# Output projection: norm factors moved from the operand to the products, and weight-block sums made early and kept in DRAM

## The chip, the cores and the metric

The kernel runs on one core of one Trainium2 chip. The metric is the device time of one execution in microseconds (us). The core has a matrix engine (TensorE, PE in the profile), a vector engine (VectorE, DVE), an activation engine (ScalarE, ACT), a general engine (GpSimd, POOL) and SyncE (SP), whose queue issues all of this kernel's DMA transfers. Each engine works through its own instructions in order and waits on semaphores for the others.

## The reference

One layer of a decoder trunk in float32: 2048 tokens, model width 1024. An input projection feeds two parallel mixers, a diagonal state-space layer with a GLU (`y_a`) and an SSD mixer (`y_b`). Each result is RMS-normalised with a gain per channel, the two are joined, and one output projection of 2048 channels maps them back to 1024. An FFN follows. The part that the change touches is the middle of this:

```python
y_a = rmsnorm(y_a, s5_norm[i])
...
y_b = rmsnorm(y_b, ssd_norm[i])
x = x + jnp.concatenate([y_a, y_b], axis=-1) @ w_out[i]
h = rmsnorm(x, norm_ffn[i])
x = x + (jax.nn.silu(h @ w_gate[i]) * (h @ w_up[i])) @ w_down[i]
```

`rmsnorm(y, g)` multiplies each token's row by one number, `rsqrt(mean(y*y) + eps)`, and each channel by its gain `g`.

## The kernel before

**Products.** Float32 products are made of three matmuls of a split operand: each operand is rounded to a high part (a copy on ACT, line 942) and the remainder is the low part (a subtraction on DVE, line 947); `split` does both. The output projection and the FFN use Winograd's form of Strassen's scheme on 2x2 blocks: seven products P1 to P7 instead of eight. For one step, `stationary_operands` makes seven operands from the token side (A11, A12, A22 and the sums S1 to S4, four sums on DVE), each 128 channels by 128 tokens in four pieces. The weight side, `Moving`, keeps seven operands (B11, B21, B22 and the sums T1 to T4) of 4 x 128 channels by 512 columns, which serve eight steps. A step is 7 x 4 x 3 = 84 matmuls of 128x128 by 128x512, all recorded at line 1126.

**The output projection, `mixed_out`.** It runs 16 steps: r = 0, 1 over the two halves of the channels (r=0 is `y_a`, read from DRAM as `yaD`; r=1 is `y_b`, `ybD`), and within each, c = 0 to 7 over groups of 256 tokens. `normed(r, c)` loads the raw tokens of the step after the present one, channels on partitions, puts the tokens' norm factors on a diagonal (`dg`, line 1173), spreads them over the partitions by a matmul with ones (`ps_iv`, line 1175), and multiplies by gain and factor with eight DVE instructions of 128x256 (line 1179). `winograd` then issues the products. Ends (line 1132) add a finished product from PSUM into the residual rows; a product that is needed further on in the same PSUM bank is first copied out by ACT (`kept`, line 1137) into one of two scratch tiles and added from there (line 1139). The first step of a row block uses another order of products, `FIRST`, than the others, `ORDER`. For r=0 the residual rows come from the input `x` and the sums go to DRAM (`xaD`); for r=1 they are loaded from `xaD`, whose rows are spread over all eight steps of r=0, and go on to the FFN.

**Weights of the output projection.** Four blocks of 1 MB of `w_out` are loaded for each r, and T1 to T4 are made of them on DVE (line 985 through `Moving.minus`, and lines 1197 and 1198 at the start). For r=0 this takes place at the start of `mixed_out`, for r=1 in `next_rows`: it loads two blocks at c=4, and hangs the rest on the products of c=7, after which the places of old operands come free. At r=1, c=4 `NextTokens` begins to prepare the operands of the FFN in half of the token buffer, which has one place for tokens from there on instead of two.

**Around it.** The GLU (`glu`) of the state-space layer ends just before: for each block of its output, ACT squares it and POOL adds the square to `sums` (line 921), from which `glu_norm` makes the norm factors `ainv` with ones-column matmuls (line 874). The SSD mixer gives `yinv` in the same way. The tiles of the output projection lie in memory that the SSD mixer's tiles leave.

**Far earlier,** at 195 to 420 us of the profiled execution, `project` runs the first half of the input projection's columns for the convolution (`xs`, 12 tiles) and the gate (`zs`, 8 tiles), two tiles in a pair. Each tile loads 0.5 MB of weights, splits them on ACT (line 66) and POOL (line 69) and has 48 matmuls; three PSUM banks take turns, and ACT evacuates them (line 718). DVE has the convolution (line 731) and, until about 240 us, the tables of the state-space layer. The five large buffers (`slots`, `k.take`) are not all in use then: number 3 is idle.

The order of each engine's instructions is set by a scheduler that lays the program out along a simulated timeline; `high_priority` and `issue_after` guide it.

Of the kernel before, what the change touches and what calls it, by code (L numbers as in the profile page):

```python
# [19 lines left out]
P = 128  # L20
# [860 lines left out]
def glu(k, ins, half, sp):  # L881
# [18 lines left out]
    for i in range(0, KD, 2):  # L900
# [5 lines left out]
        for q, (m, w, b) in enumerate(order):  # L906
# [13 lines left out]
            if m:  # L920
                nc.gpsimd.tensor_add(sums[:, b], sums[:, b], sq)
            if half and i + q == 1:
# [177 lines left out]

def winograd(k, A, B, order, scratch, C, onto, after={}):

# [10 lines left out]
    if "P4" not in chain:  # L1113
        kept["P7"] = (c21, c21)

    ends = {"P2": (c11, c21), "P3": (c12, c12), "P7": (c22, c22), "P4": (c21, c21)}
    bank = {}
    for name in order:
# [11 lines left out]
        if name in ends and (onto or name != "P4" or name not in chain):  # L1130
            dst, src = ends[name]
            V.tensor_add(dst, ps, dst if onto else src)  # L1132
            ps = None
        if name in kept:
            dst, block = kept[name]
            dst = scratch() if onto else dst
            nc.scalar.copy(dst, bank[root])  # L1137
            if onto:
                V.tensor_add(block, block, dst)  # L1139
# [4 lines left out]


def mixed_out(k, ins, sp, s):


    nc = k.nc
    V, G = nc.vector, nc.gpsimd  # L1150
    w_out = ins["w_out"][0]
    tok = lambda ap, hf, j: ap[hf * HALF : hf * HALF + HALF, :].rearrange("(c j) d -> j c d", j=8)[j]

    def load_of(r):
        def load(dst, i, j):
            row = r * D + i * 512
            nc.sync.dma_start(dst, w_out[row : row + 512, j * 512 : j * 512 + 512].rearrange("(k p) d -> p k d", p=P))

        return load

# [3 lines left out]

    def normed(r, c, behind=None):

        st = stage[:, c % 2 if r == 0 or c < 4 else 0].rearrange("p (k t) -> p k t", t=256)
        src = k.ybD[:, c * 256 : c * 256 + 256] if r else k.yaD[:, c, :]
        nc.sync.dma_start(st, src.rearrange("(k p) t -> p k t", p=P))
        dg = sp.tile([P, 2, P], F32, name="dg", tag="sq", bufs=1)  # L1170
        inv = k.yinv if r else k.ainv
        for i in range(2):
            V.tensor_scalar(dg[:, i], k.ident, inv[:, 2 * c + i : 2 * c + i + 1], None, MUL)
        ps = (k.px)([P, 256], "ps_iv")
        nc.tensor.matmul(ps, k.ones, dg.rearrange("p a b -> p (a b)"), start=True, stop=True)
        col = C_SSDN if r else C_S5N
        with k.tc.issue_after(behind) if behind else nullcontext():
            for kk in range(KD):
                V.scalar_tensor_tensor(st[:, kk], st[:, kk], k.cols[:, col + kk : col + kk + 1], ps, op0=MUL, op1=MUL)  # L1179
        return st  # L1180
# [4 lines left out]
    with k.tc.high_priority():  # L1185
        B = Moving(k, 4)
        x, y = (k.take(i, [P, 2, 4, 512], F32) for i in (s[0], 6))
        r11, r12, r22, r21 = x[:, 0], x[:, 1], y[:, 0], y[:, 1]
        load(r11, 0, 0)
        load(r12, 0, 1)  # L1190
        st = normed(0, 0)
        B.split("B11", 7, r11)
        t1 = B.split("T1", 8, r11, B.minus(r11, r12, r11))
        A = operands(st, True)
        load(r22, 1, 1)
        with k.tc.issue_after(k.last_sum):
            V.tensor_sub(r11, r22, r11)
            V.tensor_sub(r12, r22, r12)
        load(r21, 1, 0)
        B.split("T2", s[1], r11)  # L1200
        B.split("B22", s[2], r22)
        with k.tc.issue_after(t1[0]):
            B.split("B21", s[3], r21)
            B.split("T3", s[4], r12)
        t4 = B.split("T4", s[0], r21, B.minus(r21, r21, r11))
    k.spare = 6

    for r in range(2):
        after = {}
        for c in range(8):  # L1210
            first = r + c == 0
            if not first:
                A = operands(st, c == 0)
            if c < 7 or r == 0:
                st = normed(*divmod(r * 8 + c + 1, 8), t4[1] if first else None)
            if c == 4:
                if r:
                    ahead = NextTokens(k, 0, tile)
                else:
                    nextB, ops = next_rows(k, B, 4, load_of(1))  # L1220
            if c == 7:
# [7 lines left out]
            winograd(k, A, B, FIRST if c == 0 else ORDER, lambda: sp.tile([P, 512], F32, name="sg", bufs=2), [(t[:, 0], t[:, 1]) for t in xt], True, after)  # L1229
            for i in range(2):  # L1230
# [113 lines left out]
def trunk_kernel(ctx, tc, ins, out, dbg=None, upto="all"):  # L1344
# [21 lines left out]
    k.m2D = dp.tile([P, NG, P], F32, name="m2D")  # L1366
    k.m1D = dp.tile([P, NG, P], F32, name="m1D")
    k.qD = dp.tile([P, NG, P], F32, name="qD")

# [48 lines left out]
    with ExitStack() as c1:  # L1418
# [110 lines left out]
```

## Time and profile before

| | us |
|---|---|
| median of 3 runs | 3020.07 (3012.84 to 3021.89) |
| the profiled execution, its own time | 3016.45 |
| its span in the profile | 3014.7 |
| PE busy | 2833.0 (94%) |
| DVE busy | 2102.2 (70%) |
| ACT busy | 1118.2 (37%) |
| POOL busy | 535.6 (18%) |
| DMA | 398.84 MB, mean 132 GB/s |

Times within the profile are counted from its first instruction. "Idle before" is time that an engine stood still, and the name behind the arrow is what ended it. The matmuls overlap: one of 128x512 is shown with 389 ns, and the next starts well before it ends, so a PE that is busy all the time may still be held to its own pace and not by anything else. PEclk is the clock granted to PE, as a share of the full one. The output projection takes the time from 1279 us to about 1650 us.

### The profile page before, as it was taken

To read this page: it belongs to the slowest core of one execution; us is meant where nothing else is said; L and a number is where in the kernel's file an instruction comes from. 1 tells how busy PE (TensorE), PEld (TensorE's weight loads), DVE (VectorE), ACT (ScalarE), POOL (GpSimd) and SP (SyncE) were. 2 spreads that over 40 slices of the span, in tenths; PEclk is the share of its full clock that TensorE was granted. 3 is DMA by queue.
4 is the path that set the end of the run, shared out by engine and by line. 5 is a ranking of instruction groups with operands and counts; after the bars stand their busy time and mean duration, and the time that the engine had idled before them with its cause. 6 is when DMAs were issued, how large, how long until landed. Compare 5 with 4: busy or idle time off the path is not lost.

```text
span 3014.7 us, 35741 instructions
## 1 busy us (share of the span) xinstructions
PE 2833.0 (94%) x12972; PEld 2257.6 (75%) x12972; DVE 2102.2 (70%) x3953; ACT 1118.2 (37%) x1817; POOL 535.6 (18%) x462
## 2 busy tenths in 40 slices
PE   4898999999999989989899999999999999999996
PEld 3776777677787777768677788887788887878875
DVE  5586218989668888797878755556655557677686
ACT  3134322333454333332434433334333334243343
POOL 1343311114366766510000000000000000000000
PEclk8999999999999999999999999999999999999998
DMA  6455335443446454545455222233222224545444
GB/s 118 116 157 169 117 97 173 140 140 104 132 129 191 145 165 140 174 153 172 134 167 161 74 75 82 84 112 101 96 84 84 79 76 141 194 168 192 165 153 140
DMA packets 331992, 398.84 MB, mean 132 GB/s; under 512 B 49804, under 2 KB 249592, under 8 KB 331816
## 3 DMA queue, kind: packets, MB, share of 16 engines
q1 hardware_dynamic: 331816, 396.56, 42.1%
q8 instruction: 102, 1.67, 0.2%
q14 instruction: 74, 0.61, 0.1%
HBM read 264.39 MB, written 132.12 MB: 132 GB/s over the span
## 4 chain that ended last, share of the span: by engine, by line
PE 62%; DVE 19%; DMA 11%; issue 3%; ACT 2%; SPq 2%; POOL 1%; DVEq 0%; ACTq 0%; POOLq 0%
PE ps_w L1126 40%; PE ps_in L81 4%; PE ps_in L83 4%; PE ps_in L82 4%; DMA s<-ybD 2%; DVE s L947 2%; DVE acc L731 1%; DMA out_dram<-x 1%; PE ps_y L575 1%; DVE wS L947 1%; PE ps_glu L81 1%; PE ps_glu L82 1%; PE ps_glu L83 1%; DVE x L1132 1%; DVE s L1179 1%
## 5 line engine op out<-in xcount | busy, mean ns | idle before, releaser
L1126 PE MATMUL ps_w<-s,wS 128*128 128x512 f32 x3936 | 957.7, 397 | 39.0 <-DVE s L947 16.8
L1126 PEld LDWEIGHTS ps_w<-s,wS 128*128 128x128 f32 x3936 | 747.3, 191 | 213.9 <-DVE s L947 18.8
L1126 PE MATMUL ps_w<-s,wA 128*128 128x512 f32 x2952 | 731.4, 398 | 29.8 <-DVE x L1132 10.3
L1126 PEld LDWEIGHTS ps_w<-s,wA 128*128 128x128 f32 x2952 | 558.8, 190 | 167.7 <-DVE x L1132 12.1
L81 PE MATMUL ps_in<-s,whi 128*128 128x512 f32 x896 | 353.5, 395 | 9.1 <-ACT xp L718 9.0
L83 PE MATMUL ps_in<-s,wlo 128*128 128x512 f32 x896 | 351.8, 395 | 1.6 <-POOL wlo L69 1.6
L82 PE MATMUL ps_in<-s,whi 128*128 128x512 f32 x896 | 352.9, 394 | 0.0
L942 ACT CAST wS<-sum 128x512 fp32r<-128x512 f32 (+1 forms) x336 | 203.5, 611 | 396.7 <-PE ps_w L1126 195.6
L947 DVE TENSOR_TENSOR wS<-sum,wS 128x512 fp32r<-128x512 f32 (+1 forms) x336 | 225.5, 675 | 140.5 <-ACT wS L942 139.9
L69 POOL TENSOR_TENSOR wlo<-wst,whi 128x1024 fp32r<-128x1024 f32 x72 | 188.7, 2621 | 424.1 <-ACT whi L66 424.0
L942 ACT CAST wA<-s 128x512 fp32r<-128x512 f32 (+1 forms) x252 | 150.7, 610 | 242.0 <-PE ps_w L1126 162.1
L81 PEld LDWEIGHTS ps_in<-s,whi 128*128 128x128 f32 x896 | 169.4, 189 | 49.0 <-ACT xp L718 10.3
L83 PEld LDWEIGHTS ps_in<-s,wlo 128*128 128x128 f32 x896 | 169.4, 189 | 40.9 <-issue 3.1
L82 PEld LDWEIGHTS ps_in<-s,whi 128*128 128x128 f32 x896 | 169.4, 189 | 36.9 <-issue 2.3
L1132 DVE TENSOR_TENSOR gu<-ps_w,gu 128x512 f32<-128x512 f32 x134 | 92.5, 691 | 148.3 <-PE ps_w L1126 144.5
L803 POOL TENSOR_TENSOR s<-cm,dtas 128x512 fp32r<-128x512 f32 x128 | 161.8, 1292 | 76.0 <-PE ps_seg L804 76.0
L947 DVE TENSOR_TENSOR wA<-s,wA 128x512 fp32r<-128x512 f32 (+1 forms) x252 | 165.1, 671 | 3.2 <-ACT wA L942 3.2
L1132 DVE TENSOR_TENSOR x<-ps_w,x 128x512 f32<-128x512 f32 x160 | 108.7, 685 | 57.1 <-PE ps_w L1126 56.9
L731 DVE SCALAR_TENSOR_TENSOR acc<-xp,cols,acc 128x1024 f32<-128x1024 f32 x72 | 102.7, 1426 | 50.6 <-ACT acc L729 49.9
L66 ACT CAST whi<-wst 128x1024 fp32r<-128x1024 f32 x72 | 75.5, 1049 | 167.9 <-PE ps_in L82 99.8
L1137 ACT COPY gu<-ps_w 128x512 f32<-128x512 f32 x134 | 78.4, 586 | 141.7 <-PE ps_w L1126 141.4
L1139 DVE TENSOR_TENSOR x<-x,sg 128x512 f32<-128x512 f32 x125 | 85.0, 686 | 65.7 <-ACT sg L1137 38.5
(354 smaller groups left out, 3612.8 us busy)
## 6 DMA issues: line engine op xcount, KB each, us to landing
wst<-in_w_in_dram SPq DMA_DIRECT2D x56, 512.0 KB
s<-in_w_gate_dram SPq DMA_DIRECT2D x22, 1024.0 KB
s<-in_w_up_dram SPq DMA_DIRECT2D x22, 1024.0 KB
actD<-gu SPq DMA_DIRECT2D x44, 512.0 KB
s<-actD SPq DMA_DIRECT2D x16, 1024.0 KB
xD<-xo SPq DMA_DIRECT2D x24, 512.0 KB
uD<-ev SPq DMA_DIRECT2D x16, 512.0 KB
zD<-sz SPq DMA_DIRECT2D x32, 256.0 KB
```

The lines of the kernel that those rows point to most:

```text
L69: eng.tensor_sub(lo, st, hi.bitcast(F32))
L81: nc.tensor.matmul(ps, wh[:, i, :], rh[:, i, :], start=(i == 0), stop=False)
L82: nc.tensor.matmul(ps, wh[:, i, :], rl[:, i, :], start=False, stop=False)
L83: last = nc.tensor.matmul(ps, wl[:, i, :], rh[:, i, :], start=False, stop=(i == n - 1))
L731: V.scalar_tensor_tensor(acc, tap(i), col(i), acc, op0=MUL, op1=ADD)
L803: G.tensor_mul(r, bc(k.tri.unsqueeze(1), [P, 4, P]), bc(part, [P, 4, P]))
L942: a = k.nc.scalar.copy(op[:, 0], raw)
L947: b = eng.tensor_sub(op[:, 1, part], raw[:, part], op[:, 0, part].bitcast(F32))
L1126: nc.tensor.matmul(ps, a[:, p, i, :], b[:, q, i, :], start=(root == name and i == 0 and p + q == 0), stop=(i == n - 1 and p == 1), skip_gr ...
L1132: V.tensor_add(dst, ps, dst if onto else src)
L1137: nc.scalar.copy(dst, bank[root])
L1139: V.tensor_add(block, block, dst)
```

## The change

1. `normed` becomes `tokens`: it only loads. The token operands are made of raw tokens.
2. The norm factor of a token is applied as the products leave PSUM, where tokens lie on partitions: `winograd` gets `scale`, a factor per partition for each of the two token blocks, in the ends (a scaled add instead of an add) and in the kept copies (a scaled activation instead of a copy).
3. The channel gains go into the weights. `out_rows` loads two rows of blocks of `w_out` (0.5 MB each), scales them in place on ACT, makes T1 to T4 on DVE and stores all eight results, 2 MB, to DRAM (`woD`). It is called eight times, behind the six pairs of `xs` tiles and the first two pairs of `zs` tiles, with buffer 3, so that each call's loads wait for the store of the call before.
4. `mixed_out` loads its operands of the weight side, sums too, from `woD`: seven of 1 MB for each r instead of four blocks. `made_rows` replaces `next_rows` for r=1, with the loads of T3, T2, B22, B21 and T4 in its hooks of step c=7.
5. The last four additions of squares in the GLU of the second half are done by DVE instead of POOL.

```diff
@@ glu @@
             if m:
-                nc.gpsimd.tensor_add(sums[:, b], sums[:, b], sq)
+                (V if half and i == KD - 2 else nc.gpsimd).tensor_add(sums[:, b], sums[:, b], sq)
@@ winograd @@
-def winograd(k, A, B, order, scratch, C, onto, after={}):
+def winograd(k, A, B, order, scratch, C, onto, after={}, scale=None):
...
+    row = {"P2": 0, "P3": 0, "P7": 1, "P4": 1}
+    row_kept = {"P1": 0, "P6": 0, "P5": 1, "P7": 1}
...
-            V.tensor_add(dst, ps, dst if onto else src)
+            if scale:
+                V.scalar_tensor_tensor(dst, ps, scale[row[name]], dst, op0=MUL, op1=ADD)
+            else:
+                V.tensor_add(dst, ps, dst if onto else src)
...
-            nc.scalar.copy(dst, bank[root])
+            if scale:
+                nc.scalar.activation(dst, bank[root], AF.Identity, scale=scale[row_kept[name]])
+            else:
+                nc.scalar.copy(dst, bank[root])
@@ new functions @@
+OPS = ("B11", "B12", "B21", "B22", "T1", "T2", "T3", "T4")
+def out_rows(k, w_out, r, kk):
+    nc, V = k.nc, k.nc.vector
+    t = k.take(3, [P, 8, 512], F32)
+    for i in range(2):
+        b = t[:, 2 * i : 2 * i + 2].rearrange("p a n -> p (a n)")
+        row = r * 8 + i * 4 + kk
+        nc.sync.dma_start(b, w_out[row * P : row * P + P, :])
+        nc.scalar.activation(b, b, AF.Identity, scale=k.cols[:, C_S5N + row : C_S5N + row + 1])
+    b11, b12, b21, b22, t1, t2, t3, t4 = (t[:, i] for i in range(8))
+    V.tensor_sub(t1, b12, b11)
+    V.tensor_sub(t2, b22, t1)
+    V.tensor_sub(t3, b22, b12)
+    V.tensor_sub(t4, b21, t2)
+    nc.sync.dma_start(k.woD[r, kk], t)
+def made_rows(k, old, load):
+    m = Moving(k, 4)
+    x = k.spare
+    t = k.take(x, [P, 2, 4, 512], F32)
+    load(t[:, 0], "B11")
+    load(t[:, 1], "T1")
+    r = {}
+    def p1():
+        m.split("B11", old.at["B11"], t[:, 0])
+        load(t[:, 0], "T3")
+    def p2():
+        k.spare = old.at["B21"]
+        r["y"] = k.take(k.spare, [P, 2, 4, 512], F32)
+        load(r["y"][:, 0], "T2")
+        load(r["y"][:, 1], "B22")
+    def p6():
+        m.split("T1", old.at["T2"], t[:, 1])
+        load(t[:, 1], "B21")
+    def p5():
+        m.split("T2", old.at["T1"], r["y"][:, 0])
+        load(r["y"][:, 0], "T4")
+    def p4():
+        m.split("B21", old.at["T4"], t[:, 1])
+        m.split("T4", x, r["y"][:, 0])
+    return m, { ... "P7": split of "B22", "P3": split of "T3" ... }
@@ mixed_out @@
-    def normed(r, c, behind=None):
+    def tokens(r, c):
...
         nc.sync.dma_start(st, src.rearrange("(k p) t -> p k t", p=P))
-        dg = sp.tile([P, 2, P], F32, name="dg", tag="sq", bufs=1)
-        inv = k.yinv if r else k.ainv
-        for i in range(2):
-            V.tensor_scalar(dg[:, i], k.ident, inv[:, 2 * c + i : 2 * c + i + 1], None, MUL)
-        ps = (k.px)([P, 256], "ps_iv")
-        nc.tensor.matmul(ps, k.ones, dg.rearrange("p a b -> p (a b)"), start=True, stop=True)
-        col = C_SSDN if r else C_S5N
-        with k.tc.issue_after(behind) if behind else nullcontext():
-            for kk in range(KD):
-                V.scalar_tensor_tensor(st[:, kk], st[:, kk], k.cols[:, col + kk : col + kk + 1], ps, op0=MUL, op1=MUL)
         return st
...
-        t1 = B.split("T1", 8, r11, B.minus(r11, r12, r11))
+        B.split("T1", 8, x[:, 1])
         A = operands(st, True)
-        load(r22, 1, 1)
-        with k.tc.issue_after(k.last_sum):
-            V.tensor_sub(r11, r22, r11)
-            V.tensor_sub(r12, r22, r12)
-        load(r21, 1, 0)
-        B.split("T2", s[1], r11)
...
-        t4 = B.split("T4", s[0], r21, B.minus(r21, r21, r11))
+        load(x[:, 0], "T3")
+        load(x[:, 1], "B21")
+        B.split("T2", s[1], y[:, 0])
+        load(y[:, 0], "T4")
+        B.split("B22", s[2], y[:, 1])
+        B.split("T3", s[4], x[:, 0])
+        B.split("B21", s[3], x[:, 1])
+        t4 = B.split("T4", s[0], y[:, 0])
...
-                    nextB, ops = next_rows(k, B, 4, load_of(1))
+                    nextB, ops = made_rows(k, B, load_of(1))
@@ trunk_kernel @@
-        project(k, 0, h, xs)
+        todo = [(r, kk) for r in range(2) for kk in range(4)]
+        for _ in project_pairs(k, 0, h, xs):
+            out_rows(k, ins["w_out"][0], *todo.pop(0))
...
-            project(k, 0, h, zs)
+            for _ in project_pairs(k, 0, h, zs):
+                if todo:
+                    out_rows(k, ins["w_out"][0], *todo.pop(0))
```

More of the change, by code (lines that the diff above doesn't have):

```diff
@@ L1143, in winograd @@
     return ps
+OPS = ("B11", "B12", "B21", "B22", "T1", "T2", "T3", "T4")
[37 more added lines that the diff above has]
+        m.split("T4", x, r["y"][:, 0])
+    return m, {
+        "P1": p1,
+        "P2": p2,
+        "P6": p6,
+        "P5": p5,
+        "P7": lambda: m.split("B22", old.at["T3"], r["y"][:, 1]),
+        "P3": lambda: m.split("T3", old.at["B22"], t[:, 0]),
+        "P4": p4,
+    }
 def mixed_out(k, ins, sp, s):
@@ L1150, in mixed_out @@
     V, G = nc.vector, nc.gpsimd
-    w_out = ins["w_out"][0]
     tok = lambda ap, hf, j: ap[hf * HALF : hf * HALF + HALF, :].rearrange("(c j) d -> j c d", j=8)[j]
     def load_of(r):
[L1155 to L1159, printed above, removed]
+        return lambda dst, name: nc.sync.dma_start(dst, k.woD[r, :, :, OPS.index(name)].rearrange("k p n -> p k n"))
     load = load_of(0)
@@ L1187, in mixed_out @@
         x, y = (k.take(i, [P, 2, 4, 512], F32) for i in (s[0], 6))
[L1188 to L1192, printed above, removed]
-        t1 = B.split("T1", 8, r11, B.minus(r11, r12, r11))
-        A = operands(st, True)
-        load(r22, 1, 1)
-        with k.tc.issue_after(k.last_sum):
-            V.tensor_sub(r11, r22, r11)
-            V.tensor_sub(r12, r22, r12)
-        load(r21, 1, 0)
-        B.split("T2", s[1], r11)
[L1201 to L1204, printed above, removed]
-        t4 = B.split("T4", s[0], r21, B.minus(r21, r21, r11))
+        load(x[:, 0], "B11")
+        load(x[:, 1], "T1")
+        st = tokens(0, 0)
+        load(y[:, 0], "T2")
+        load(y[:, 1], "B22")
+        B.split("B11", 7, x[:, 0])
+        B.split("T1", 8, x[:, 1])
+        A = operands(st, True)
+        load(x[:, 0], "T3")
[6 more added lines that the diff above has]
+        t4 = B.split("T4", s[0], y[:, 0])
     k.spare = 6
@@ L1209, in mixed_out @@
         after = {}
+        inv = (k.ainv, k.yinv)[r]
         for c in range(8):
@@ L1214, in mixed_out @@
             if c < 7 or r == 0:
-                st = normed(*divmod(r * 8 + c + 1, 8), t4[1] if first else None)
+                st = tokens(*divmod(r * 8 + c + 1, 8))
             if c == 4:
@@ L1228, in mixed_out @@
                 nc.sync.dma_start(xt[i].rearrange("p a n -> p (a n)"), rows(k.xaD, 2 * c + i) if r else tok(k.x, i, c))
-            winograd(k, A, B, FIRST if c == 0 else ORDER, lambda: sp.tile([P, 512], F32, name="sg", bufs=2), [(t[:, 0], t[:, 1]) for t in xt], True, after)
+            winograd(k, A, B, FIRST if c == 0 else ORDER, lambda: sp.tile([P, 512], F32, name="sg", bufs=2), [(t[:, 0], t[:, 1]) for t in xt], True, after, [inv[:, 2 * c + i : 2 * c + i + 1] for i in range(2)])
             for i in range(2):
@@ L1367, in trunk_kernel @@
     k.m1D = dp.tile([P, NG, P], F32, name="m1D")
+    k.woD = dp.tile([2, 4, P, 8, 512], F32, name="woD")
     k.qD = dp.tile([P, NG, P], F32, name="qD")
```

## The prediction

> **What bounds the kernel now.** I read the page first: TensorE (PE) is busy nearly everywhere, so only its stalls and its own instructions can be saved.
>
> ```profile
> span 3014.7 us, 35741 instructions
> PE 2833.0 (94%) x12972; PEld 2257.6 (75%) x12972; DVE 2102.2 (70%) x3953; ACT 1118.2 (37%) x1817; POOL 535.6 (18%) x462
> ```
>
> Then I cut the stretches that the diff touches into stages: start of the output projection, its steady part, the change of row block, the tail into the FFN, and (last two) the convolution and gate columns of the first input projection, where the new early work goes.
>
> ```profile
> core 0: us, PE busy (x) PEld busy (x) DVE busy (x) ACT busy (x) POOL busy (x), PEclk, DMA share, GB/s
> 1279.00:1333.00 54.00, 40.77 (x152) 30.95 (x151) 54.00 (x91) 23.27 (x35) 12.49 (x3) 0.87 0.53 175
> 1333.00:1463.00 130.00, 130.00 (x569) 106.45 (x567) 107.16 (x200) 46.55 (x76) 0.00 (x0) 1.00 0.46 159
> 1463.00:1530.00 67.00, 55.43 (x217) 42.18 (x217) 56.14 (x114) 25.09 (x42) 0.00 (x0) 0.95 0.51 136
> 1569.00:1681.00 112.00, 97.08 (x416) 75.81 (x415) 96.88 (x206) 50.70 (x82) 0.00 (x0) 0.94 0.45 141
> 195.00:335.00 140.00, 126.91 (x602) 101.29 (x601) 94.88 (x122) 59.10 (x82) 56.87 (x61) 0.98 0.51 152
> 335.00:375.00 40.00, 40.00 (x178) 33.10 (x177) 3.86 (x3) 9.85 (x13) 9.57 (x4) 1.00 0.35 119
> ```
>
> At the start VectorE (DVE) is busy for all 54.00 us and PE only 40.77: DVE is the bound there. In the steady part PE is full, and DVE's 107 of 130 is cover. In the other two stages PE lacks 11.6 and 14.9 us. Last, PE's own pace (timeline):
>
> ```profile
> 1339.24 9.49 PE L1126 MATMUL ps_w<-s,wS 128*128 128x512 f32 x41
> 1348.57 2.91 PE L1126 MATMUL ps_w<-s,wA 128*128 128x512 f32 x12
> 1355.69 0.59 PE L1175 MATMUL ps_iv<-dg,cm 128*128 128x256 f32 x2
> 1355.94 2.21 PE L1126 MATMUL ps_w<-s,wA 128*128 128x512 f32 x8
> ```
>
> Columns are start, length, engine and line, with the count last. 41 matmuls take 9.33 us from start to start: 0.228 each, so a step of 84 takes 19.1. The two ps_iv records take 0.25, and the 8 matmuls behind them 2.21, where 12 take 2.91 and 8 would take 2.00: 0.46 us for one `normed`.
>
> **The change, part by part.** First the durations of what goes and comes (groups of 1260 to 1660 us, with count, busy us and mean ns; below them operations of the tiles ps_w and ps_t, with least, median and greatest ns):
>
> ```profile
> L1179 DVE SCALAR_TENSOR_TENSOR s<-s,cols,ps_iv 128x256 f32<-128x256 f32 x128 | 52.4, 473 | 33.7 <-DMA s<-ybD 28.4 <-DMA s<-yaD 4.9 <-PE ps_w L1126 0.3
> L947 DVE TENSOR_TENSOR wS<-sum,wS 128x512 fp32r<-128x512 f32 x68 | 45.8, 682 | 0.0
> L1132 DVE TENSOR_TENSOR x<-ps_w,x 128x512 f32<-128x512 f32 x63 | 42.8, 683 | 6.7 <-PE ps_w L1126 6.6
> L985 DVE TENSOR_TENSOR s<-s,s 128x1024 f32<-128x1024 f32 x8 | 9.4, 1218 | 0.4 <-DMA s<-in_w_out_dram 0.4
> L1173 DVE TENSOR_SCALAR dg<-cm,ainv 128x128 f32<-128x128 f32 x14 | 3.4, 278 | 1.1 <-PE ps_iv L1175 1.1
> L947 DVE TENSOR_TENSOR s<-s,s 128x1024 fp32r<-128x1024 f32 x32 | 37.9, 1216 | 2.2 <-ACT s L942 2.2
> L1197 DVE TENSOR_TENSOR s<-s,s 128x2048 f32<-128x2048 f32 x1 | 2.3, 2278 | 0.0
> L1137 ACT COPY sg<-ps_w x125: 564/587/600, 1291.9 to 2994.1; 128x512 f32<-128x512 f32 x125
> L152 ACT ACTIVATE s<-ps_t,cols x16: 680/687/713, 1642.3 to 2108.0; 128x512 fp32r<-128x512 f32 x16
> L155 DVE SCALAR_TENSOR_TENSOR s<-ps_t,cols,s x16: 736/740/750, 1584.4 to 2113.9; 128x512 f32<-128x512 f32 x16
> ```
>
> *Per step.* Each of 16 `normed` calls loses 8 x 0.473 + 2 x 0.278 = 4.3 us of DVE and 0.46 of PE. Added: four ends as scaled adds (like L155, 0.74, for L1132, 0.68) and three or four kept copies as scaled activations (like L152, 0.69, for 0.59): 0.24 us of DVE and at most 0.4 of ScalarE (ACT), under PE's 19.1. DVE starts its next instruction some 0.08 before the end of one, so a 128x512 one counts 0.6. Seven operand splits (the 128x512 L947), four sums and seven evacuations make 18 x 0.6 = 10.8; DVE's need per step falls from 15.1 to 11.0 us.
>
> *Start.*
>
> ```profile
> 1267.07 7.73 DMA s<-yaD
> 1278.75 0.40 PE L83 MATMUL ps_glu<-s,wlo 128*128 128x512 f32 x1
> 1316.03 3.58 PE L1126 MATMUL ps_w<-s,wA 128*128 128x512 f32 x15
> ```
>
> The first row, of the chain of waits, is the load of the first tokens; in the others (PE's timeline) the GLU matmuls end and the 84th matmul of step 0 falls. DVE work that leaves before 1333: three `normed` (13), T1 and T4 as four L985 of 1.2 (4.9), L1197 and its twin (4.6): 22 us. Added: four adds of the GLU sums at 0.68 (2.7) and the ends (0.5). Net 19 us of a full engine. PE doesn't get all of it: its GLU matmuls end at 1279, and A11 waits for the token load, which lands at 1274.8 now as then. Counting DVE from there: seven operand splits and four sums (6.6), five B splits of two L947 (11.7), three gate products and the four adds of the GLU (4.5), statistics of the norms (5, an allowance), evacuations of the step (4.5): done at 1307, against 1318.5 now. T3, B21 and T4 are loaded into buffers that the splits of B11, T1 and T2 free; SP waits for these, and behind it stand GLU stores, x and token loads, which are needed a step later and cost nothing while a step lasts longer than one wait. I take 12 us (bounds 4, if each B operand waits for its load, and 19, all of DVE's relief).
>
> *GLU sums from POOL to DVE.* PE stands behind them, in order, and so do the x loads that reuse their buffers:
>
> ```profile
> PE ps_ss L874 <- POOL suma L921: 6.3, 2, 3.6
> 1266.76 1.28 POOL L921 TENSOR_TENSOR suma<-suma,gs 128x512 f32<-128x512 f32 x1 [1.29 <-ACT gs L919]
> 1288.63 5.41 POOL L921 TENSOR_TENSOR suma<-suma,gs 128x512 f32<-128x512 f32 x1 [3.70 <-ACT gs L919]
> ```
>
> The add takes 1.28 us beside an idle DVE and 5.41 beside a full one; 0.68 on DVE. The 6.3 us lie inside the start's bounds; what is late next is the square on ACT behind DVE's own gate product.
>
> *Steady.* 9 steps that PE fills, 0.46 each: 4 us.
>
> *Change of row block.* DVE loses four T subtractions (8 x 1.2 = 9.6) and 4.3 per step. But the residual rows of r=1 are loaded from what r=0's last step stores:
>
> ```profile
> 1467.57 2.61 DMA xaD<-x
> 1470.92 10.22 DMA x<-xaD
> ```
>
> That chain stays: with two scratch tiles PE can do five products (13.7 us) before it needs x. Seven operands of 1 MB come where four blocks came. Of these five fall into the last step: 5.2 MB in 19.1 us is 274 GB/s on the steady 159, more than the most seen,
>
> ```profile
> 1270.00:1280.00 10.00, 9.58 (x43) 7.61 (x41) 7.90 (x16) 5.15 (x7) 0.00 (x0) 1.00 1.02 362
> ```
>
> so about 1.4 MB, 3.8 us, is late and delays x. Of 11.6 us idle and some 3 at a low clock (PEclk 0.95 of 67 us) I take back 7 (bounds -4 and 13).
>
> *Tail.* From c=4 of r=1 the tokens have one buffer, and load, scaling and splitting follow each other (chain of waits):
>
> ```profile
> 1563.17 10.06 DMA s<-ybD
> 1573.26 3.06 DVE s L1179 x8
> 1590.81 10.18 DMA s<-ybD
> 1612.19 9.62 DMA s<-ybD
> ```
>
> Loads begin 27.6 and 21.4 us apart, more than 19.1. Without the 3 us of scaling most of that fits. In the same stage one stall stays, since DVE makes the FFN's operands there (timeline, idle time in brackets):
>
> ```profile
> 1673.90 2.50 PE L1126 MATMUL ps_w<-s,wS 128*128 128x512 f32 x5 [5.55 <-DVE s L947]
> ```
>
> Of the 14.9 us idle 9 are left to win. I take 7 (bounds 2 and 12, with time at a low clock).
>
> *Early work.* Eight times: two loads of 0.5 MB, two ACT scalings of 128x1024 (no row has them; at most two of L152, 1.4), four subtractions (0.68) and a store of 2 MB; 22 us of DVE, at most 22 of ACT and 25 MB in all. Two lie in the gate columns, where DVE is busy 3.86 of 40 us: nothing. Six lie in the convolution columns, one per pair (21.9 us of PE): 3.1 MB more is 144 GB/s on 152, 296 in all, under 362. All DMAs share SP's queue, so a weight load can stand behind a 2 MB store (5.8 us), and ACT can stand before a late load. What the trace shows of that kind:
>
> ```profile
> PE ps_in L81 <- ACT xp L718: 9.0, 3, 5.9
> PE ps_in L83 <- POOL wlo L69: 1.6, 2, 1.5
> ACT junk L171 <- DMA xb<-in_x_dram: 17.6, 7, 5.4
> ```
>
> The 4 MB of x blocks held ACT 17.6 us, and PE 9.0. Three PSUM banks of 5.5 us cover a wait of some 11. Bounds: 0, and 9.0 per 4 MB for 19 MB, 40 us. I take 4, near the lower end, because the early loads are spread over 140 us and the x blocks came together.
>
> A rule speaks against this part: the Trainium skill, "SBUF — State Buffer" ("Who interferes with whom"), has VectorE with two SBUF inputs and GpSimd hold a shared port pair exclusively, the loser waiting for the whole instruction. The 5.41 us add agrees. By it 24 subtractions could hold up POOL's weight splits by 16 us, and were all that PE's, 14 us would be saved instead of 26.
>
> **Sum.** 12 + 4 + 7 + 7 - 4 = 26 us less. The profiled execution took 3016.45 us, 1.75 beyond its span, and gives 2990; it stands 3.6 below the median of the three runs, 3020.07, so 2994 for a median.
>
> A rule would add to it: by "TensorE: Matmul & The Clock Gate" (Part 1) of the Trainium skill an idle time over some 3.4 us halves PE's clock. The row at 1673.90 agrees, with 500 ns a matmul instead of 228. My takings count no such time at the start; there it could give 2 to 3 us more.
>
> **The rivals.**
> 1. *Transfers take DVE's place.* Fourteen operands of 1 MB instead of eight blocks of w_out and their subtractions. If each B operand lands no sooner than DVE used to finish it, start 4 and row block -4 remain: 4 + 4 - 4 + 7 - 4 = 7 less, 3013. For: 362 GB/s at 1270, and the 433 asked for in the last step. Against: share 0.46 to 0.53 around it.
> 2. *Slower: early work blocks the input projection.* SP or ACT, in order, stands before a w_out load or DVE's subtractions while weights or PSUM wait. It decides from 5 us per pair (30 gained, over six); at 7 it costs 42: 3029. For: the 17.6 us of ACT before x blocks. Against: PE is busy 127 of 140 in spite of them, and DVE only 95.
> 3. *All stalls go.* The 13.2, 11.6 and 9 of the 14.9 us, the time at a low clock (some 8) and 7.4 of ps_iv: about 49 less, 2971.
> 4. *It does nothing for the start:* PE's order puts the ps_ss matmuls ahead of DVE's late adds, and PE waits as long. 12 becomes 2: 3004.
>
> **How the numbers follow.** Forecast (10 to 40 less): 0.57; rival 1: 0.14; rival 2: 0.13; rival 3: 0.08; rival 4: 0.08. The three runs spread over 9.05 us, so 0.3% is about what can be told from no change. Faster: 0.57, 0.08, 0.08 and a quarter of rival 1, 0.76; same: 0.12; slower: 0.12. Range 2968 to 3015: rivals 3 and 4 and half of rival 1 inside, rival 2 and the rest out.
>
> **What would show it.** Right: no ps_iv records; DVE no longer full from 1279 to 1333 and c=0 of r=0 done some 12 us sooner; token loads under 20 us apart in r=1; PE idle in the convolution columns within 5 us of today's 13. Wrong: PE waiting there for weight splits or for evacuations behind w_out loads; operand splits waiting for woD; x of r=1 landing later behind B21 and T4.

## The result, and the profile after

The changed kernel takes 3004.5 us (median of 7 runs, 2996.41 to 3006.62) against 3020.07 of the kernel before on the same chip (7 runs, 3012.84 to 3025.21): a ratio of 0.9945, with a 95% interval of 0.9931 to 0.9959. That is 15.6 us less. The forecast was 26 less, 2994; the range held the time. The profiled execution took 2999.95 us, 16.5 below that of before.

The page of the changed kernel, its span and the busy times of the engines:

```profile
span 2998.2 us, 35602 instructions
PE 2822.7 (94%) x12940; PEld 2251.7 (75%) x12940; DVE 2060.0 (69%) x3815; ACT 1137.4 (38%) x1833; POOL 536.2 (18%) x458
```

The 32 ps_iv matmuls are gone (12972 to 12940), and DVE is busy for 42 us less, although it has 22 us of new subtractions. Next the stretches that answer to those cut from the trace of before: start, steady part, change of row block, tail, and the convolution and gate columns. The bounds are moved with the ends of the stages.

```profile
core 0: us, PE busy (x) PEld busy (x) DVE busy (x) ACT busy (x) POOL busy (x), PEclk, DMA share, GB/s
1290.00:1332.00 42.00, 34.12 (x145) 26.80 (x144) 37.67 (x71) 24.19 (x36) 0.00 (x0) 0.92 0.83 296
1332.00:1445.00 113.00, 113.00 (x495) 92.72 (x494) 71.06 (x109) 36.79 (x61) 0.00 (x0) 1.00 0.46 155
1445.00:1527.00 82.00, 77.06 (x328) 62.24 (x327) 63.82 (x120) 40.51 (x62) 0.00 (x0) 0.98 0.70 216
1527.00:1636.00 109.00, 102.34 (x463) 82.42 (x462) 81.78 (x192) 47.29 (x78) 0.00 (x0) 0.98 0.55 173
195.00:350.00 155.00, 131.39 (x631) 104.47 (x630) 116.54 (x150) 65.23 (x91) 67.61 (x66) 0.93 0.65 194
350.00:390.00 40.00, 40.00 (x178) 33.12 (x177) 3.85 (x3) 10.23 (x14) 9.57 (x4) 1.00 0.35 119
```

In the projection PE now lacks 7.9, 0, 4.9 and 6.7 us, and DVE is full nowhere. But in the convolution columns PE lacks 23.6 us, where it lacked 13.1. The account by stages, from the timelines of the two profiled executions (first gate evacuation; last ps_glu matmul; for the ends of the steps, DVE's last add of a product into the residual rows; first copy of the FFN's products):

| | before | after | measured | predicted |
|---|---|---|---|---|
| first gate evacuation | 334.1 | 349.6 | +15.5 | +4 |
| from there to the GLU's last matmul | 944.7 | 940.6 | -4.0 | 0 |
| start: GLU's end to the end of c=1, r=0 | 67.5 | 55.3 | -12.2 | -12 |
| steady: c=2 to 6 | 102.8 | 99.2 | -3.6 | -4 |
| change of row block: c=7 of r=0 to c=2 of r=1 | 94.1 | 82.3 | -11.8 | -7 |
| tail: c=3 to the first FFN copy | 111.6 | 108.6 | -3.0 | -7 |
| the rest | 1360.0 | 1362.6 | +2.6 | 0 |

The projection gained 30.6 us where 30 were forecast. The early work lost 15.5 where 4 were forecast.

**Where the 15.5 us went.** PE's waits from 70 to 350 us (total, times, longest), the kernel after:

```profile
PE ps_in L81 <- ACT whi L66: 10.9, 1, 10.9
PE ps_in L81 <- ACT xp L718: 9.0, 3, 5.5
PE ps_in L83 <- POOL wlo L69: 5.8, 4, 2.3
```

One wait of 10.9 us is new, and the waits for POOL's weight splits grew from 1.6 to 5.8. Counted in `ps_in` matmuls, PE was level with the kernel before up to the one that started there at 290 us, and 15.1 us behind at the one that started there at 316: nearly all of the loss arises in that short stretch. The long wait is followed back in four timelines of the kernel after. PE stands still until ACT has cast a block of weights (start, length, engine and line, idle time and what ended it):

```profile
313.17 0.39 PE L83 MATMUL ps_in<-s,wlo 128*128 128x512 f32 x1
324.42 0.79 PE L81 MATMUL ps_in<-s,whi 128*128 128x512 f32 x1 [10.86 <-ACT whi L66]
```

ACT reaches that cast late, because the squares of the next x blocks stand ahead of it in its queue, and each waits for its load:

```profile
314.81 1.06 ACT L171 ACTIVATE junk<-xb 128x1024 bf16<-128x1024 f32 x1 [4.42 <-DMA xb<-in_x_dram]
...
318.68 1.06 ACT L171 ACTIVATE junk<-xb 128x1024 bf16<-128x1024 f32 x1 [1.11 <-DMA xb<-in_x_dram]
...
322.28 1.06 ACT L171 ACTIVATE junk<-xb 128x1024 bf16<-128x1024 f32 x1 [2.45 <-DMA xb<-in_x_dram]
323.25 0.19 ACT L171 ACTIVATION_READ_ACCUMULATOR junk<-xb 128x1 f32 x1
323.34 1.03 ACT L66 CAST whi<-wst 128x1024 fp32r<-128x1024 f32 x1
```

On SP these loads follow the last store of the state-space tables (`m2D`):

```profile
276.90 5.16 SPq L483 DMA_DIRECT2D m2D<-Ks  x8
...
283.38 3.27 SPq L169 DMA_DIRECT2D xb<-in_x_dram  x5
...
287.20 16.44 SPq L169 DMA_DIRECT2D xb<-in_x_dram  x3
```

In the kernel before they are 28 us earlier:

```profile
249.18 4.87 SPq L483 DMA_DIRECT2D m2D<-Ks  x8
255.53 1.33 SPq L169 DMA_DIRECT2D xb<-in_x_dram  x2
```

And the tables are late because DVE makes them, and the subtractions of `out_rows` stand among their instructions. The first one holds DVE still for 22.5 us, with table code (L322, L329) on both sides of it:

```profile
66.22 0.22 DVE L322 SCALAR_TENSOR_TENSOR c<-c,r 128x64 f32<-128x64 f32 x1
88.97 0.69 DVE L1168 TENSOR_TENSOR s<-s 128x512 f32<-128x512 f32 x1 [22.53 <-ACT s L1166]
89.58 0.22 DVE L329 TENSOR_TENSOR sn<-sn,m 128x64 f32<-128x64 f32 x1
```

(That wait by itself turns out to be cheap: e8 and e9 below have it too.) Later, where DVE has no idle time left, subtractions (L1168 to L1171) stand between the tables' own instructions (L445 to L462):

```profile
236.50 1.21 DVE L445 TENSOR_TENSOR W<-B,RV 128x1024 f32<-128x1024 f32 x1
237.64 0.68 DVE L1168 TENSOR_TENSOR s<-s 128x512 f32<-128x512 f32 x1
238.25 1.34 DVE L462 TENSOR_TENSOR W<-W,tq 128x1152 f32<-128x1152 f32 x1
...
243.04 0.68 DVE L1170 TENSOR_TENSOR s<-s 128x512 f32<-128x512 f32 x1
243.64 0.68 DVE L1169 TENSOR_TENSOR s<-s 128x512 f32<-128x512 f32 x1
244.24 1.21 DVE L446 TENSOR_TENSOR tq<-B,RV 128x1024 f32<-128x1024 f32 x1
```

So the steps do not lie at 195 to 375 us, as the prediction had it. The scheduler drew them forward: their loads start between 76.8 and 228.4 us, and from 160 to 260 us DVE is busy 95.4 of 100 us (89.8 before). A chain of DVE, SP, ACT and PE carries the delay on, each link an engine that works in order.

### The profile page after: what moved, and what is told of

Same layout as the page of the kernel before. It is cut to its first block, busy times and chain, and to the rows that moved or that the text cites. A ratio compares the mean times of both kernels' runs of the same rounds, so it can differ in the third digit from the quotient of the medians.

```text
span 2998.2 us, 35602 instructions
## 1 busy us (share of the span) xinstructions
PE 2822.7 (94%) x12940; PEld 2251.7 (75%) x12940; DVE 2060.0 (69%) x3815; ACT 1137.4 (38%) x1833; POOL 536.2 (18%) x458
## 4 chain that ended last, share of the span: by engine, by line
PE 62%; DVE 18%; DMA 12%; issue 3%; ACT 2%; SPq 2%; POOL 0%; DVEq 0%; ACTq 0%; POOLq 0%
PE ps_w L1128 42%; PE ps_in L81 4%; PE ps_in L82 3%; PE ps_in L83 3%; DMA s<-ybD 2%; DVE s L947 2%; DVE acc L731 2%; DMA out_dram<-x 1%; PE ps_y L575 1%; DMA wst<-gD 1%; PE ps_yd L817 1%; PE ps_glu L81 1%; DMA s<-in_w_out_dram 1%; DMA ybD<-E 1%; DVE wS L947 1%
## 5 line engine op out<-in xcount | busy, mean ns | idle before, releaser
L81 PE MATMUL ps_in<-s,whi 128*128 128x512 f32 x896 | 356.8, 399 | 23.2 <-ACT whi L66 10.9
L731 DVE SCALAR_TENSOR_TENSOR acc<-xp,cols,acc 128x1024 f32<-128x1024 f32 x72 | 111.1, 1543 | 35.1 <-ACT acc L729 34.7
L947 DVE TENSOR_TENSOR s<-s,s 128x1024 fp32r<-128x1024 f32 (+1 forms) x90 | 103.6, 1179 | 6.3 <-ACT s L942 6.3
```

The source lines that it names most:

```text
L81: nc.tensor.matmul(ps, wh[:, i, :], rh[:, i, :], start=(i == 0), stop=False)
L731: V.scalar_tensor_tensor(acc, tap(i), col(i), acc, op0=MUL, op1=ADD)
L947: b = eng.tensor_sub(op[:, 1, part], raw[:, part], op[:, 0, part].bitcast(F32))
```

## The experiments

The table gives for each kernel, from its profiled execution in us, the issue of the last `m2D` store and of the first x-block load, the longest PE wait for a cast, the first gate evacuation, and the time from the GLU's last matmul to the first FFN copy with its four stages as above.

| | last m2D | first x load | cast wait | first gate | GLU to FFN | start | steady | change | tail |
|---|---|---|---|---|---|---|---|---|---|
| before | 249.2 | 255.5 | - | 334.1 | 376.0 | 67.5 | 102.8 | 94.1 | 111.6 |
| after | 276.9 | 283.4 | 10.9 | 349.6 | 345.4 | 55.3 | 99.2 | 82.3 | 108.6 |
| e3 no early work | 246.3 | 252.7 | - | 334.8 | 352.3 | 55.5 | 99.2 | 84.5 | 113.2 |
| e4 norm half | 246.5 | 252.9 | - | 334.3 | 368.7 | 65.8 | 100.4 | 92.5 | 110.1 |
| e10 weights half | 275.6 | 282.0 | 12.3 | 349.1 | 361.3 | 57.8 | 99.9 | 88.5 | 115.1 |
| e11 sums on POOL | 277.4 | 283.8 | 11.5 | 351.3 | 348.1 | 57.1 | 99.2 | 82.2 | 109.6 |
| e7 no subtractions | 265.4 | 271.5 | 0.8 | 332.1 | 347.0 | 55.9 | 99.2 | 83.7 | 108.2 |
| e8 no transfers | 270.3 | 277.0 | - | 337.2 | 345.3 | 55.1 | 99.2 | 80.4 | 110.6 |
| e9 four and four | 261.7 | 268.0 | 0.8 | 334.3 | 345.1 | 54.6 | 99.2 | 81.8 | 109.5 |

Each row is a single execution. Seven kernels (after, e1, e2, e5, e6, e7, e9) have the same code for the output projection, and their values still spread: the start over 54.3 to 56.7, the change of row block over 81.7 to 85.7, the tail over 108.2 to 116.2 and the whole over 344.8 to 354.3. The gains at the start and at the change of row block are well clear of that. The 3.0 of the tail are not.

**e1 and e2: a hold that did not bind.** The steps were to move into the gate columns (e1) or to be spread (e2).

```diff
+                with tc.issue_after(k.gemm.ins):
+                    for _ in range(2):
                         out_rows(k, ins["w_out"][0], *todo.pop(0))
```

> The changed kernel, with the early work held back to the gate columns: two blocks of rows behind each of the four pairs of gate tiles, each held until that pair's last matmul is issued. Theory A (the early work costs some 15 us because the scheduler pulled it forward to 77 to 247 us, among the tables, where VectorE is full): the convolution columns end as early as in the kernel before (first gate evacuation at 334 instead of 350 us), and the total is 13 to 16 us less than the changed kernel's, 2988 to 2992. Theory B (25 MB more of transfers cost what they cost, wherever they are): the gate columns grow by as much as the convolution columns shrink, and the total stays within 4 us of 3004. In both the gate columns ask for some 405 GB/s for 88 us, more than the 362 seen, so that a few us of loss there are possible.

> As the run before, but spread wider: one block of rows behind each of the last three pairs of convolution tiles, then two, one, one and one behind the gate pairs, held in the same way. Theory A: 2 to 6 us behind the run before if any of it lies beside the tables (they end near 260 us), otherwise the same, 2988 to 2995. Theory B: within 4 us of 3004.

e1 took 3001.5 us (6 runs), ratio 0.9948 (0.9934 to 0.9963); e2 3004.68, 0.996 (0.9946 to 0.9973). `k.gemm` is a matmul of PE, and the loads, which are SP's, were not held by it: they started at 74.5 and 73.5 us, as in the changed kernel. Both runs say nothing on the question, except that the changed kernel's time repeats.

**e3: no early work.** No `out_rows`; `load` takes the raw blocks of `w_out` by the first four names, twice, so gains and sums are left out. The transfers of the projection are as many as in the changed kernel.

> The changed kernel without the early work: nothing of the weights is scaled or summed, and the seven operands of the weight side are loaded as plain blocks of w_out, so gains and sums are left out. Both theories: the whole early cost goes, and the output projection keeps its gain of 30 us: 2988 to 2991. If the total stays near 3004, the 15 us in the convolution columns are not the early work's (theory C: the new order of the whole program, not the work, costs them).

It took 2989.86 us, 0.9911 (0.9896 to 0.9925), and its first gate evacuation lies at 334.8. So the 15 us are the early work's, and they would be saved if that work were hidden. (The profiled run was the longest of the five, 2996.25, so its 352.3 need not be a loss in the projection.)

**e4 and e10: each half alone.** e4 is the kernel before with norm factors on the products (`tokens`, `scale`), gains left out, weights and T1 to T4 made as before. e10 is the changed kernel with `normed` put back:

```diff
-                st = tokens(*divmod(r * 8 + c + 1, 8))
+                st = normed(*divmod(r * 8 + c + 1, 8), t4[1] if first else None)
```

> The kernel before with the norm factors applied to the products only: raw tokens, scaled ends and kept copies; the weights are loaded and summed in the output projection as in the kernel before (the channel gains are left out). It removes 16 x 4.3 us of VectorE and 16 x 0.46 us of TensorE and leaves the T sums. By the prediction's terms (steady 4, tail 7, and of the start 13 of 22 us and of the row block change 8.6 of 18 us of VectorE): 4 + 7 + 7 + 3 = 21 less than before, 2999. If the sums made early carried most of the gain (rival), 8 or less below before, 3012 or more.

> Edit: the gains and sums of weight blocks are made early as in the changed kernel, but the tokens are normed before their split as in the kernel before (broadcast matmul and eight DVE instructions for each step; the channel factors are applied twice, so the output is not the reference's). Beside e4 it tells whether the two halves add. Theory that they add: of the 30.6 us that the projection lost, the norm alone gave about 7, so this gives 23, less 11 to 15 for the early work: GLU to first FFN copy 351 to 356, time 3003 to 3010. Rival (either half alone leaves DVE the bound at the start and at the change of row block, so that most of the gain needs both): GLU to FFN 364 to 370, time 3016 to 3024.

e4 took 3011.52 us, 0.9974 (0.9963 to 0.9985): GLU to FFN 7.2 us shorter. Its theory, the prediction's terms, had 21 less. It came out 6.9 less than the kernel before of its own runs, as the rival had it (8 or less, if the sums made early carry most of the gain). e10 took 3015.72, 0.9995 (0.9986 to 1.0004): 14.7 shorter, and 13.3 lost before the GLU ends. Neither e10's theory (351 to 356) nor its rival (364 to 370) named the 361.3. The halves give 21.9 us one by one and 30.6 together. By the table the start comes from the weights (9.7 of 12.2), and the change of row block needs both: 1.6 and 5.5 alone, 11.8 together. e4 still has PE waiting for POOL's sums (waits, 1240 to 1340 us):

```profile
PE ps_ss L874 <- POOL suma L921: 8.2, 2, 4.1
```

**e11: the GLU's last sums back on POOL.**

```diff
-                (V if half and i == KD - 2 else nc.gpsimd).tensor_add(sums[:, b], sums[:, b], sq)
+                nc.gpsimd.tensor_add(sums[:, b], sums[:, b], sq)
```

> Edit: the last two sums of squares of the GLU go back to POOL; everything else is as in the changed kernel. Theory (the sums' way to the norm factors no longer sets the start, since the operands now wait for loads and not for the factors): same time as the changed kernel within 2 us, 3000 to 3005. Rival (the ps_ss matmuls stand in PE's queue ahead of the first products, as the prediction had it): PE waits 4 us at each of the two sums, and the time is 3007 to 3012.

3007.4 us, 0.9969 (0.9958 to 0.998): some 3 us slower than the changed kernel by the medians, and 5 when each is set against the kernel before of its own runs. The time lies in the rival's range, but not for its reason: no PE wait at ps_ss is left. Nor is the difference clear of noise: e2, which keeps the sums on DVE, has 0.996 (0.9946 to 0.9973), and e11's rows in the table lie within or close to the spread given there. What the sums alone are worth, if anything, is not shown.

**e5 and e6: steps held in earnest.** `k.stored` is the last store of a gate or convolution tile, an instruction of SP.

```diff
+                with tc.issue_after(k.stored.ins):
+                    for _ in range(2):
                         out_rows(k, ins["w_out"][0], *todo.pop(0))
```

> Edit: the eight row blocks are made in the gate columns alone, two to a pair of columns, and their loads are queued on SP behind the last store of the pair before, so that none can start before the first gate store. Everything else is as in the changed kernel. Theory A (the cost of about 15 us comes from ACT and DVE instructions that stand among the state-space tables, where DVE has no idle time): the first gate evacuation comes back to about 335 us (before 334.1, changed 349.6), the gate columns, where DVE has room, grow by 2 to 5 us, and the time is 2989 to 2994. Theory B (the 25 MB of loads and stores cost, wherever they lie): the gate stage of some 55 us has to carry them beside its own, the gain at the first gate evacuation is given back by the end of the gate columns, and the time is 2999 to 3006. Theory C (one wait at the end of the convolution columns, the cast of the next block behind the x-block squares on ACT, is moved by a new order): the time falls by 5 to 8 us only, to about 2997.

> Edit: the row blocks are held on SP as in e5, but one behind the fifth and one behind the sixth pair of convolution columns, and then two, two, one and one behind the pairs of gate columns. Theory A: two blocks among the last convolution columns, where DVE is still full, cost 2 to 4 us, the gate columns less than in e5: 2990 to 2996. Theory B: the load on the transfers is more even than in e5, so this is the better of the two, and by 3 to 8 us. Theory C: as e5, about 2997.

e5 took 3035.41 us, 1.0053 (1.0035 to 1.0071), e6 3020.87, 1.0007 (0.9995 to 1.002). Theory A was right on its place: e5's first gate evacuation is at 333.6, and the gate columns carried four steps with PE full. But no theory had counted the round trip of one step. Eight steps share buffer 3, so each loads only when the store of the one before has landed (e5, SP's timeline, loads and stores of the fourth to the last step):

```profile
399.66 0.86 SPq L1165 DMA_DIRECT2D s<-in_w_out_dram  x2
410.61 0.33 SPq L1172 DMA_DIRECT2D woD<-s  x1
417.36 0.86 SPq L1165 DMA_DIRECT2D s<-in_w_out_dram  x2
428.00 0.33 SPq L1172 DMA_DIRECT2D woD<-s  x1
...
464.35 0.80 SPq L1165 DMA_DIRECT2D s<-in_w_out_dram  x2
472.44 0.33 SPq L1172 DMA_DIRECT2D woD<-s  x1
```

From 350.29 to 464.35 are seven trips, 16.3 us each on average (14.3 to 18.1). The stage has room for four; the operands of the next block of tokens, made behind it (`ps_t`), then wait for the buffer (e5, PE's waits from 400 to 500 us):

```profile
PE ps_t L120 <- DVE s L139: 48.6, 3, 47.6
```

In e6, whose steps start earlier, this wait is 22.9 us.

**e7 and e8: the early work without its subtractions, and without its transfers.**

```diff
# e7
-    V.tensor_sub(t1, b12, b11)
...
-    nc.sync.dma_start(k.woD[r, kk], t)
+    nc.sync.dma_start(k.woD[r, kk, :, 0:4], t[:, 0:4])
+    nc.sync.dma_start(k.woD[r, kk, :, 4:8], t[:, 0:4])
# e8
+    if r + kk == 0:
+        k.early = k.take(3, [P, 8, 512], F32)
...
-        nc.sync.dma_start(b, w_out[row * P : row * P + P, :])
-    nc.sync.dma_start(k.woD[r, kk], t)
```

> Edit: the four subtractions of blocks in each of the eight steps are left out (the four sums are then copies of the blocks, stored with as many bytes), so 32 DVE instructions of about 0.6 us each fewer, some 20 us of DVE; the loads, the channel factors on ACT and the stores stay where they were. What is computed in the projection is not the reference's. Theory A, with DVE as the engine: the first gate evacuation comes 12 to 15 us sooner, at 335 to 338, and the time is 2989 to 2993. Theory A with ACT as the engine, or theory B: no change, 3001 to 3006. Theory C: between, 2996 to 3000.

> Edit: only the first of the eight steps loads its rows, and none stores; all eight do their scalings on ACT and subtractions on DVE on that one tile, and the projection loads raw blocks of the weights in place of the ones made. The 24 MB of transfers of the early work are left out but for 1 MB; what is computed is not the reference's. Theory A: the cost stays, first gate evacuation 345 to 350, time 3000 to 3006. Theory B: it goes, first gate evacuation 335 to 338, time 2989 to 2993. If both this kernel and e7 regain it in part, the cost is of both kinds.

2990.9 us, 0.9907 (0.9889 to 0.9925), and 2989.07, 0.9906 (0.9889 to 0.9923): each regains everything, where theory A had this for e7 alone and theory B for e8 alone. With no transfers to wait for, the subtractions of e8 were all over by 132.7 us, ahead of the stretch from 160 us on where DVE has no idle time; with the transfers alone DVE has nothing new to do.

The tables show what is left of that. DVE ends each of the eight with L479. The first of these comes 10.9 us later in the changed kernel than in the kernel before, and 8.4, 13.3 and 4.7 later in e7, e8 and e9; so the long wait at the first subtraction, 22.4 us in e8 and 21.5 in e9, is mostly swallowed by idle time that DVE had in the kernel before (busy 2.9 of 30 us from 130 to 160). From the first to the last L479 it is 85.7 us before, 91.4 in e7, e8 and e9, and 102.5 in the changed kernel, where twelve subtractions of 8.3 us in all stand in between. (The 5.7 us that e7, e8 and e9 have on the kernel before go with three more of the convolution's adds, L731, in the same stretch.) What costs is thus a subtraction held back by its transfers until DVE has no room. And the loss is not in proportion: x loads that start at 268 to 271.5 instead of 255.5 cost nothing at the first gate column, 277.0 costs 3, and 280.7 to 284 (e1, e2 and e12 among them) cost 14 to 17.

**e9: the same work, four steps early and four late.**

```diff
+        for i, _ in enumerate(project_pairs(k, 0, h, xs)):
+            with tc.issue_after(k.stored.ins) if i > 3 else nullcontext():
+                out_rows(k, ins["w_out"][0], *todo.pop(0))
```

and the remaining two in the same way behind the first two gate pairs.

> Edit: the first four of the eight steps stay free (in the changed kernel their subtractions are over by 150 us), the last four are queued on SP behind stores of the last convolution columns and the first gate columns. Same instructions and same bytes as in the changed kernel. Theory (a step costs only where its four DVE instructions, and the waits for its loads ahead of them, stand in the queue of a DVE with no idle time, here 160 to 260 us): the first gate evacuation comes at 334 to 339 us instead of 349.6, no long wait of PE follows at the end of the gate columns because only four round trips of about 16 us are left for 320 to 400 us, and the time is 2987 to 2993. Rival (loads, scalings and stores cost their 15 us wherever they lie, and the kernels without subtractions and without transfers regained it for reasons of their own): 2999 to 3006.

It took 2990.32 us (5 runs, 2986.98 to 2995.86), 0.991 (0.9898 to 0.9922), as little as the kernel without early work, and 14 us less than the changed kernel. Every instruction and byte is kept. The last table store is issued at 261.67 and the x loads at 267.97 (SP's timeline):

```profile
261.67 4.88 SPq L483 DMA_DIRECT2D m2D<-Ks  x8
...
267.97 11.36 SPq L169 DMA_DIRECT2D xb<-in_x_dram  x8
```

PE's waits of the same kernel, 70 to 440 us, do not have the long one:

```profile
PE ps_in L83 <- POOL wlo L69: 8.5, 5, 3.0
PE ps_in L81 <- ACT xp L718: 7.9, 3, 3.6
...
PE ps_in L81 <- ACT whi L66: 0.8, 1, 0.8
```

The late steps start at 318.0, 343.5, 362.9 and 380.3, the last store is issued at 391.3, and PE is full from 335 to 410 us beside them. This version beats both kernels.

**e12: shorter token loads in the tail.**

```diff
+        if r and c > 3:
+            nc.sync.dma_start(st[:, 0], src[0:P])
+        else:
             nc.sync.dma_start(st, src.rearrange("(k p) t -> p k t", p=P))
```

> Edit: in the second row block, the token loads of steps c=4 to 7 bring only the first of the four blocks of 128 channels (0.25 MB instead of 1 MB; the other three keep older tokens, so the output is not the reference's). In the changed kernel these four loads take 8 to 10 us, and each starts only when the operand A22 has been split into its one buffer, behind the last product of the step before; ACT waits 17.1 us for them between 1530 and 1640. Theory (the tail's gain stayed at 3 us because the length of these loads, not the scaling that was removed, sets the steps of the tail): the tail, from the end of step c=2 to the first FFN copy, falls from 108.6 to 98 to 104 us, and the time to 2994 to 3000. Rival 1 (PE's own extra work in the tail, the transposes for the FFN, and the stall at the FFN's first operands set it, the loads lie beside it): the tail stays within 2 us, time 3002 to 3006. Rival 2 (with the loads short, the stall moves to the FFN's first operands): the steps c=4 to 7 are shorter by 5 to 10 us, but PE's wait before the FFN, now 5.6 us, grows by as much, and the time stays at 3002 to 3006.

2998.8 us, 0.9944 (0.9931 to 0.9958), the ratio of the changed kernel. (The time lies in the theory's range, but the kernel before took only 3015.89 beside it.) The tail takes 106.5 us instead of 108.6: steps c=5 and 6 gained 3.6, and part of that was lost again before the FFN. The theory, which had the tail at 98 to 104, falls. The loads are late, but the stall that remains is at the FFN's first operands, with long loads (after) and short ones (e12):

```profile
1655.21 2.50 PE L1128 MATMUL ps_w<-s,wS 128*128 128x512 f32 x5 [5.63 <-DVE s L947]
```

```profile
1655.37 2.50 PE L1128 MATMUL ps_w<-s,wS 128*128 128x512 f32 x5 [5.62 <-DVE s L947]
```

## Why the prediction was right, and where it was not

The range held the time, and the direction came from the causes that were named for the projection. The size is less well founded than 15.6 inside 10 to 40 looks. The 30.6 for 30 in the projection is partly luck, since 4.8 more at the change of row block and 4 less in the tail cancel; and the early work cost four times its term. The time also fell on rival 4's number, 3004, for other reasons than rival 4's. (By its own terms rival 2's 42 us would give a median of 3032; the 3029 goes by the profiled execution.)

*Start, 12 forecast, 12.2 measured.* DVE was the bound and is so no longer. e10 shows which part of the relief counts: four T's that are not made there. Of the list of what would show it, "c=0 done some 12 us sooner" came as 7.4 in c=0 and 4.8 in c=1, counted from the GLU's end, so the total agrees better than its parts. Only 5.3 of the 12.2 are idle time of PE (13.2 us before, 7.9 after); most of the rest goes with PE's clock, 0.90 before and 0.94 after in this stage, and with three `normed` (1.3) that are gone. Rival 4 did not come: of PE's 6.3 us of waits at ps_ss 0.4 are left.

*Steady, 4 and 3.6.* These two do not count the same steps: the prediction has nine, the row five. On PE's timeline one `normed` cost 0.44 us, as forecast (0.46), which is 2.2 us for the five; the other 1.4 come from how far DVE's last add lags behind PE at the two ends of the row. The durations were right too: the scaled add takes 0.75 us (estimate 0.74), the scaled kept copy 0.69 (0.69).

*Change of row block, 7 and 11.8.* PE's idle time fell from 11.6 to 4.9 us; four `normed` (1.8) and PE's clock (0.96 before, 0.98 after) give most of the rest. The failed step is the term for late transfers, 3.8 us. Five operands did fall into one step (SP, kernel after: issues of several loads in one row):

```profile
1442.88 1.61 SPq L1225 DMA_DIRECT2D s<-woD  x3
...
1451.89 5.70 SPq L1225 DMA_DIRECT2D s<-woD  x2
...
1465.20 1.27 SPq L1283 DMA_DIRECT2D x<-xaD  x2
```

but the 362 GB/s that the prediction took for the most is no ceiling, although the DMA engines were busy throughout that window too (share 1.02). Here the rate in 40 slices of 1430 to 1500 us was:

```profile
GB/s 374 33 0 9 0 241 59 9 201 405 406 384 334 400 385 375 389 384 399 138 19 236 159 134 196 171 233 186 129 104 184 152 133 61 243 173 377 345 145 145
```

Ten slices of 1.75 us, from 1445.75 on, have a mean of 386. PE is full from 1443 to 1466 us. What came late for PE is not x (DVE waited 4.1 us for it, until 1477.7, and PE did not), but the token load behind it, and that cost PE one wait of 2.2 us (chain of waits, kernel after):

```profile
1469.57 16.45 DMA s<-ybD
1486.05 0.69 DVE sum L1086
...
1488.15 0.70 ACT sg L1143
```

*Tail, 7 and 3.0.* The failed step is "Without the 3 us of scaling most of that fits". Token loads now start 24.5 and 21.8 us apart, not under 20 as listed, since each still waits until A22 of the step before has been split. And there was less behind it than the prediction thought: as the account above cuts the tail, PE had 8.4 us idle before and has 6.7 now, and with short loads (e12) the tail is only 2 us shorter. By the spread of the same code, 108.2 to 116.2 us, even the 3.0 are not sure. The steps there also hold work of PE's own, 60 transposes for the FFN with 8.4 us of busy time in 1530 to 1640 us.

*Early work, 4 and 15.5.* Two things failed. "Six lie in the convolution columns, one per pair" read the place from the program's order, while the scheduler puts an instruction where its inputs and buffer allow, 120 us earlier. And "22 us of DVE" were costed at nothing because DVE had time over on average; the stretch in which they came had none. The listed signs of the wrong course came: waits for weight splits (10.9 and 5.8 us), and 23.6 us of PE idle where 13 within 5 was to be right. Rival 2 had the right engines, SP or ACT standing before what others need, but took the loads of `w_out` to be in front; it was the x blocks, behind tables that DVE finished late. That rival's threshold, 5 us per pair, was not reached; the loss was a single one.

*The rule on the shared ports.* By the Trainium skill, "SBUF — State Buffer" ("Who interferes with whom"), the subtractions could hold POOL's weight splits up by an estimated 16 us. POOL's row in the convolution columns (195 to 350 us), kernel after:

```profile
L69 POOL TENSOR_TENSOR wlo<-wst,whi 128x1024 fp32r<-128x1024 f32 x11 | 34.1, 3096 | 54.2 <-ACT whi L66 54.2
```

A split takes 3.10 us, against 2.84 in 195 to 335 us of the kernel before (11 as well): 2.8 us in all. Only eight of the 32 subtractions, 5.5 us, lie in that stretch, so the direction agrees there and the size is about half of them. Among the other 24, from 70 to 195 us, a split takes 2.52 us against 2.56 before: there nothing was lost. In e9 POOL's waits cost PE 8.5 us, and the first gate column was on time.

*The rule on the clock.* By "TensorE: Matmul & The Clock Gate" (Part 1) of the Trainium skill a long idle time halves PE's clock. Behind the 10.86 us wait the next seven matmuls start 0.43 us apart and then 0.23, so it cost 1.4 us more; PEclk of the columns fell from 0.98 to 0.93. The prediction's 500 ns at 1673.90 is a length divided by five, with the last matmul's overlap in it; from start to start these too are 0.43 us apart.

**What stays open.** That the x loads follow the tables' last store by 6.2 to 6.7 us in every kernel of the table is shown; whether SP's order or the memory of the tables holds them was not tried. The 4.0 us that come back between the gate columns and the GLU's end, and the 2.6 lost in the FFN, are not explained.

## What to carry to other kernels

Before work is called hidden, find out where the scheduler will put it, and look at the engine it needs in that stretch and not over the whole run: the same eight steps cost 15 us with half of them in the stretch where DVE was full, and nothing as four before it and four after it. When a delay shows up far from its cause, follow it back queue by queue; here each of four engines working in order passed it on, and slack swallowed the first 16 us of it. When steps share one buffer, count the round trips against the room before moving them.

## What the hardware showed that was not expected

Transfers, of 1 MB operands above all, ran at 386 GB/s for 17.5 us, and at up to 406 in a slice, with PE full beside them; the kernel before had shown 362 in 10 us, with its DMA engines no less busy (share 1.02, here 1.05). One step of load, scaling, subtraction and store of 2 MB took 14.3 to 18.1 us from load to load, 16.3 on average, when the steps were held to the gate columns (e5).
